# Moving the sigmoid-weighted gates of a conformer/attention block from the convolution stage into the attention stage, on one NeuronCore

## The chip, the core and the metric

The kernel runs on one core of a Trainium2 chip. A core has a matmul engine (TensorE, "PE" in the profile; "PEld" is its loading of stationary operands), a vector engine (VectorE, "DVE"), an activation engine (ScalarE, "ACT"), GpSimd ("POOL") and a sync engine (SyncE, "SP"), which here only issues DMAs. Each engine runs its own list of instructions in order and waits on semaphores for the others. The metric is the device time of the one core in microseconds. Three runs of the kernel before the change took 1415.45, 1418.73 and 1419.97 us; the median is 1418.73.

## The reference

One layer, in fp32, on 1024 latent tokens and 256 context tokens of width 1024. Weights are split per branch from one input projection:

```python
h = rms_norm(x, g_pre) * (1.0 + sc) + sh               # adaLN modulation
ua, gate_a, q, k, v, gate_b, gm = split_proj(h @ w_in)
o = latent_attention(rope(rms_norm(q)), k_all, v_all)  # 16 heads, 4 kv heads, 1280 keys
y_attn = (o * silu(gate_b)) @ w_attn_out
a, g = split(ua)
y = depthwise_conv31(a * sigmoid(g)) + conv_b
y = silu(layer_norm(y, ln_g, ln_b)) * silu(gate_a)
y_conv = y @ w_conv_out
ga, gb = split(gm)
out = (sigmoid(ga) * y_conv + sigmoid(gb) * y_attn) @ w_out
x_new = x + gt * rms_norm(out, g_post)
```

## The kernel before

**Products.** fp32 products are made of three reduced-precision ones: an operand is split into a high part (ScalarE casts it, `whi`) and a low part (source minus high part, `wlo`, by VectorE or GpSimd), and `mm3` adds high*high, low*high and high*low in PSUM. Everything is held with channels on the 128 partitions and 512 tokens (half of the sequence) in the free dimension.

**Jobs and units.** The large input projection is a list of *jobs*. A job is 128 output channels; it has two halves of 512 tokens; a half is eight *units*, and a unit is one `mm3`, three matmuls of 128x512 (`proj`). So a job has 16 units. A half accumulates in one of two PSUM buffers (`ppj` in the rows) and is taken out by an *evacuation* after its eighth unit; the half after the next one can't start before that. There are four kinds of evacuation:

- convolution gate (`gate` in `conv_jobs`): ScalarE takes the tanh (`ts<-ppj`);
- convolution value (`value`): VectorE multiplies (`y<-ts,ppj`), and the 31 taps of the depthwise convolution of those channels are put in a list, `taps`;
- silu (`silu_job`, for `gate_a` into the DRAM tile `gaD` and for `gate_b` into `gbD`): ScalarE takes the tanh, then VectorE does (tanh + 1) * value from PSUM (`ts<-ts,ppj`), then SyncE stores;
- tanh (`tanh_job`, for the merge gates `gm`, into `tgaD` and `tgbD`): ScalarE takes the tanh, then SyncE stores. VectorE has no part in it.

`stream` runs the jobs one after the other and prefetches the weights of one job: two DMAs of 256 KB (`wraw`, two buffers), two casts, two low parts on the engine in `wl[0]` (`wparts`, lines 142 to 160). `filler(n)` runs n units, `pump(n)` issues n taps, and `work(n)` does n units with taps at a fixed rate.

**Stages.** In order: modulation and the first jobs (to about 80 us); the context's keys and values; the weights of the first attention group (`group_w(0)`, line 587: four pairs of DMAs, a cast `wgh` and a low part `wgl` for each); 16 steps of queries, keys and values (four groups `g`, four quarters `q`), each with 20 units of the projection between its parts; then the rest of the units up to number 464, while the taps run out; then the PSUM is dealt out anew (`pump(len(taps))`, `unshare(2)`, `share({"o": 1})`, `share({"s": 5})`, lines 1441 to 1444): the two banks in which VectorE gathers the convolution (`pconv`) become part of the five buffers `ps` of the scores; then the maxima of the first window, and the attention proper: 16 windows of 20 steps, each with two score matmuls, an exponential on ScalarE, sums on GpSimd and VectorE, maxima of the next window on VectorE, and one unit of projection. The normalisation of the convolution's output and its gate (`ln_var`, `z_prep`) run beside the attention and read `gaD`; `gate_load` reads `gbD` for each pair of heads. After the attention comes the output: two levels of block products by a scheme with seven products for eight, and the last norm.

**What sets the order.** From the start up to the end of the 16 steps the four engines keep the order of the program text (`held = True`); after that (line 1429 on) a scheduler orders the instructions of each engine by priority, and what stands under `urgent()` comes early. SyncE's DMAs are ordered by the scheduler throughout.

**Order of the jobs.** 45 jobs are made in `early` (line 1316 on): 14 for the convolution with ten others dealt in between them, and the rest after them. The 15 silu jobs come first among the others, and the 16 tanh jobs after them; the first 29 jobs are units 0 to 464, so all silu jobs are through before the PSUM is dealt out anew, and all tanh jobs come after it, mostly in the attention.

Of the kernel before, what the change touches and what calls it, by code (L numbers as in the profile page):

```python
# [22 lines left out]
KD = 8  # L23
# [11 lines left out]
def block_kernel(ctx: ExitStack, tc: tile.TileContext, x, cx, cc, wmod, bmodT, bmodg, vecs, gpost,  # L35
# [18 lines left out]
    PE, V, S, G = (Ordered(e) for e in (nc.tensor, nc.vector, nc.scalar, nc.gpsimd))  # L54
# [7 lines left out]
    def nm(s):  # L62
        cnt[0] += 1
        return f"{s}_{cnt[0]}"

    def tl(tag, shape, bufs, dtype=F32, pool="sb"):
        return pools[pool].tile(list(shape), dtype, tag=tag, bufs=bufs, name=nm(tag))

    def opened(name, side="left"):
        p = tc.tile_pool(name=nm(name), bufs=1, side=side, reuse_waits="tile")  # L70
        pools[name] = p.__enter__()
        return p
# [35 lines left out]
    def split(hi, lo, src, he=None, le=None):  # L108
        if he is V or he is G:
            he.tensor_copy(hi, src)  # L110
        else:
            S.copy(hi, src)
        return (le or V).tensor_tensor(out=lo, in0=src, in1=f32(hi), op=ALU.subtract)
# [28 lines left out]
    wl = [G]  # L142
# [17 lines left out]
    def proj(w, rhs, hf, evac, tag="pj"):  # L160

        his, los = w
        p = pt(tag)
        for k in range(KD):
            mm3(p[:], his[k // 4][:, k % 4, :], los[k // 4][:, k % 4, :], rhs[k][0][hf][:], rhs[k][1][hf][:],
                k == 0, k == KD - 1)
            if k == KD - 1:
                with urgent():
                    evac(p, slice(hf * 512, hf * 512 + 512))
            yield  # L170
# [287 lines left out]
    def rope_tables():  # L458
        tcos, tsin = tl("blk", (P, NT, 32), 4, pool="A"), tl("blk", (P, NT, 32), 4, pool="A")
        SP.dma_start(out=tcos[:], in_=rcos)  # L460
        SP.dma_start(out=tsin[:], in_=rsin)
        gq = tl("blk", (P, NT, 32), 4, pool="A")[:, 0:4, :].rearrange("p (i a) b -> p i (a b)", i=2)
        SP.dma_start(out=gq[:, 0, :], in_=qg.partition_broadcast(P))
        SP.dma_start(out=gq[:, 1, :], in_=kg.partition_broadcast(P))
        yield 6
        for i in range(2):
            CC = tl("rope", (P, NT, HD), 4, pool="A")
            SS = tl("rope", (P, NT, HD), 4, pool="A")
            for hh in range(2):
                a, b = hh * 32, (1 - hh) * 32  # L470
                V.tensor_tensor(out=CC[:, :, a:a + 32], in0=tcos[:, :, 0:32],
                                in1=gq[:, i, a:a + 32].unsqueeze(1).to_broadcast([P, NT, 32]), op=ALU.mult)
                V.scalar_tensor_tensor(out=SS[:, :, a:a + 32], in0=tsin[:, :, 0:32], scalar=(1.0 if hh else -1.0),
                                       in1=gq[:, i, b:b + 32].unsqueeze(1).to_broadcast([P, NT, 32]),
                                       op0=ALU.mult, op1=ALU.mult)
                yield 2
            rope.append((CC, SS))
# [7 lines left out]
    gaD = [dram.tile([P, T], F32, name=nm("gaD")) for _ in range(KD)]  # L485
    tgaD = [dram.tile([P, T], F32, name=nm("tgaD")) for _ in range(KD)]
    tgbD = [dram.tile([P, T], F32, name=nm("tgbD")) for _ in range(KD)]
    ogD = [dram.tile([P, T], F32, name=nm("ogD")) for _ in range(KD)]
    gbD = [dram.tile([P, T], F32, name=nm("gbD")) for _ in range(KD)]
# [97 lines left out]
    def group_w(g):  # L587
        gw[g] = [], []
        raws = []

        def load(k):
            raws.append(tl("wgr", (P, 2, 384), 4, pool="wg"))
            SP.dma_start(out=raws[-1][:, :, 0:128], in_=wkv[:, k:k + 2, g * 128:(g + 1) * 128])
            SP.dma_start(out=raws[-1][:, :, 128:384], in_=wq[g, :, k:k + 2, :])
        for k in range(0, KD, 2):
            load(k)
        yield 6 if g else 10
        for k in range(0, KD, 2):
            hi, lo = tl("wgh", (P, 2, 384), 4, F32R, "wg"), tl("wgl", (P, 2, 384), 4, F32R, "wg")
            split(hi[:], lo[:], raws[k // 2][:], le=G if g else V)  # L600
            for i in range(2):
                gw[g][0].append(hi[:, i, :])
                gw[g][1].append(lo[:, i, :])
            yield 2 if g else 4
# [244 lines left out]
    def tanh_job(src, dst):  # L849
        def ev(p, tok):  # L850
            t = tl("ts", (P, 512), 4)
            S.activation(t[:], p[:], AF.Tanh, scale=0.5)
            SP.dma_start(out=dst[:, tok], in_=t[:])
        return src, lambda w, hf: proj(w, hT, hf, ev)

    def silu_out(p, dst):
        t = tl("ts", (P, 512), 4)
        S.activation(t[:], p[:], AF.Tanh, scale=0.5)
        V.scalar_tensor_tensor(out=t[:], in0=t[:], scalar=1.0, in1=p[:], op0=ALU.add, op1=ALU.mult)
        SP.dma_start(out=dst, in_=t[:])  # L860

    def silu_job(src, dst):
        return src, lambda w, hf: proj(w, hT, hf, lambda p, tok: silu_out(p, dst[:, tok]))
# [279 lines left out]
    def conv_out_job(j):  # L1143
        def ev(p, tok):
            t = tl("ts", (P, 512), 4)
            SP.dma_start(out=t[:], in_=tgaD[j][:, tok])
            V.scalar_tensor_tensor(out=t[:], in0=t[:], scalar=1.0, in1=p[:], op0=ALU.add, op1=ALU.mult)
            SP.dma_start(out=mcD[j][:, tok], in_=t[:])
        return wco[j], lambda w, hf: proj(w, zt, hf, ev)
# [163 lines left out]
                fin(*{2: (0, 1), 3: (1, 5), 4: (2, 7)}[n])  # L1313


    gate_jobs = [silu_job(wch[16 + j], gaD[j]) for j in range(1, KD)]
    gate_jobs += [silu_job(wch[24 + j], gbD[j]) for j in range(KD)]
    tanh_jobs = [tanh_job(wch[32 + j], tgaD[j]) for j in range(KD)]
    tanh_jobs += [tanh_job(wch[40 + j], tgbD[j]) for j in range(KD)]
    early = gate_jobs[0:1]  # L1320
    for j in range(1, KD):
        early += conv_jobs(j)
        for _ in range(2 - j % 2):
            early.append(gate_jobs[len(early) - 2 * j])
    early += gate_jobs[len(early) - 2 * (KD - 1):] + tanh_jobs
    zjobs = [conv_out_job(j) for j in range(KD)]
    NF = 16 * len(early)
    nj = len(early)
# [13 lines left out]
    def filler(n):  # L1342
        done[0] += n
        return run(fill, n)
# [3 lines left out]
    def work(n):  # L1348

        for _ in range(n):  # L1350
            filler(1)
            owed[0] = min(owed[0] + RATE, 3.0)
            while owed[0] >= 1:
                pump(1)
                owed[0] -= 1
# [18 lines left out]
    closed(stp)  # L1374
    app = opened("A")
    wgp = opened("wg")
    bg = rope_tables()
    next(bg)
    ones_rows()
    for d in group_w(0):  # L1380
        work(d)
    prev = None
    per = (NF - done[0] - NB - 72) // 16
# [2 lines left out]
    for g in range(NG):  # L1386
        for q in range(4):
# [14 lines left out]
            for i in range(per):  # L1402
# [13 lines left out]
                if i == due:  # L1416
                    d = next(bg, None)
# [11 lines left out]
    closed(app)  # L1429
    for e in (V, S, G):  # L1430
        e.held = False
    wl[0] = V
    bpp = opened("B")
    load_group(0)
    for w in range(2):
# [20 lines left out]
    score(0, 0)  # L1456
    score(0, 1)

    late = {}

    def later(step, gen):
# [15 lines left out]
    for i in range(2 * NS):  # L1477
# [24 lines left out]
        for g in late.pop(i, []):  # L1502
            with tc.issue_after(crit[0].ins), urgent():
                d = next(g, None)
# [113 lines left out]
```

## Time and profile before

| | us |
|---|---|
| median of three runs | 1418.73 (1415.45 to 1419.97) |
| the profiled execution | 1418.84 |
| its span, first to last instruction | 1417.0 |
| what lies around the span | 1.84 |
| TensorE busy | 1353.8 (96% of the span) |
| VectorE busy | 1028.2 (73%) |
| ScalarE busy | 565.1 (40%) |
| GpSimd busy | 699.7 (49%) |
| mean granted TensorE clock | 0.987 of full speed |

A busy share of 96% says that TensorE is the bound on average. The places where it is not are read from three views: the waits of TensorE in a stretch of the span (who it waited for, the sum, how often, the longest), the table by stretches of time with the granted clock beside the busy time, and the instructions in order of time, in which a bracket at the end of a row gives the idle time before it and the instruction that ended it. A granted clock of 0.50 means that the engine ran at 1.2 GHz instead of 2.4.

### The profile page before, as it was taken

To read this page: it belongs to the slowest core of one execution; us is meant where nothing else is said; L and a number is where in the kernel's file an instruction comes from. 1 tells how busy PE (TensorE), PEld (TensorE's weight loads), DVE (VectorE), ACT (ScalarE), POOL (GpSimd) and SP (SyncE) were. 2 spreads that over 40 slices of the span, in tenths; PEclk is the share of its full clock that TensorE was granted. 3 is DMA by queue.
4 is the path that set the end of the run, shared out by engine and by line. 5 is a ranking of instruction groups with operands and counts; after the bars stand their busy time and mean duration, and the time that the engine had idled before them with its cause. 6 is when DMAs were issued, how large, how long until landed. Compare 5 with 4: busy or idle time off the path is not lost.

```text
span 1417.0 us, 19558 instructions
## 1 busy us (share of the span) xinstructions
PE 1353.8 (96%) x6520; PEld 1003.5 (71%) x6520; DVE 1028.2 (73%) x1523; ACT 565.1 (40%) x1397; POOL 699.7 (49%) x567
## 2 busy tenths in 40 slices
PE   5999899999999999799999999999999999999996
PEld 3767789897888887566656666666665655788774
DVE  4486888898988898856764666667576675449977
ACT  5541344334343432144444444444454434222233
POOL 2121247566656550046665565556546666362623
PEclk9999999999999999999999999999999999999998
DMA  9733435444444447514544444543355658699754
GB/s 340 253 112 89 138 108 164 164 141 148 138 145 147 145 140 204 157 51 134 187 154 129 128 149 147 155 146 127 112 190 161 223 186 267 215 315 343 250 188 153
DMA packets 153332, 242.45 MB, mean 171 GB/s; under 512 B 19936, under 2 KB 72716, under 8 KB 153232
## 3 DMA queue, kind: packets, MB, share of 16 engines
q1 hardware_dynamic: 139792, 218.07, 46.9%
q10 hardware_dynamic: 13440, 23.14, 5.6%
q8 instruction: 51, 0.84, 0.2%
q14 instruction: 49, 0.40, 0.1%
HBM read 161.50 MB, written 79.52 MB: 170 GB/s over the span
## 4 chain that ended last, share of the span: by engine, by line
PE 60%; DVE 13%; issue 5%; DMA 4%; POOL 4%; ACT 3%; ACTq 1%; SPq 0%; POOLq 0%; DVEq 0%
PE ppj L50 27%; PE ps L50 16%; PE po L50 15%; DVE pconv L50 5%; PE pm L50 2%; DVE qkt L50 2%; DVE t L50 1%; DVE qk L50 1%; ACT pe L50 1%; DMA wraw<-in_wch 1%; POOL wlo L50 1%; DVE r1st L50 1%; POOL y L50 1%; DVE mx L50 1%; ACT qk L50 1%
## 5 line engine op out<-in xcount | busy, mean ns | idle before, releaser
L50 PE MATMUL ppj<-t,whi 128*128 128x512 f32 x1728 | 619.6, 403 | 14.9 <-DVE ts L50 11.3
L50 PEld LDWEIGHTS ppj<-t,whi 128*128 128x128 f32 x1728 | 328.4, 190 | 120.3 <-issue 34.0
L50 PE MATMUL ppj<-t,wlo 128*128 128x512 f32 x864 | 341.7, 395 | 0.0
L50 DVE TENSOR_REDUCE mx<-ps 128x1 f32<-128x512 f32 (+1 forms) x320 | 199.7, 681 | 119.2 <-PE ps L50 118.9
L50 ACT ACTIVATE pe<-ps 128x512 f32<-128x512 f32 x320 | 188.1, 597 | 204.5 <-PE ps L50 194.2
L50 PE MATMUL ps<-r,kk 128*128 128x512 f32 (+1 forms) x640 | 202.7, 398 | 1.5 <-DMA r<-mr 1.5
L50 POOL TENSOR_TENSOR psum<-psum,pe 128x512 f32<-128x512 f32 x128 | 175.4, 1387 | 41.3 <-ACT pe L50 36.6
L50 PEld LDWEIGHTS ppj<-t,wlo 128*128 128x128 f32 x864 | 164.9, 191 | 29.7 <-issue 0.2
L50 DVE SCALAR_TENSOR_TENSOR pconv<-y,cw,pconv 128x507 f32<-128x507 f32 (+5 forms) x224 | 167.9, 749 | 15.5 <-ACT pconv L50 9.6
L50 PE MATMUL po<-pe,vt 128*64 128x512 f32 x640 | 144.4, 597 | 0.0
L50 PEld LDWEIGHTS ps<-r,kk 128*128 128x128 f32 (+1 forms) x640 | 120.9, 189 | 31.1 <-issue 1.7
L50 POOL TENSOR_TENSOR psum<-psum,part 128x512 f32<-128x512 f32 x64 | 89.8, 1405 | 97.9 <-DVE part L50 97.9
L50 PE MATMUL po<-wgh,t 128*128 128x384 f32 x512 | 132.0, 339 | 0.0
L50 POOL TENSOR_TENSOR wlo<-wraw,whi 128x512 fp32r<-128x512 f32 x59 | 79.0, 1345 | 98.3 <-ACT whi L50 79.6
L50 PEld LDWEIGHTS po<-pe,vt 128*64 128x64 f32 x640 | 43.1, 136 | 81.2 <-issue 78.9
L50 PEld LDWEIGHTS po<-wgh,t 128*128 128x128 f32 x512 | 93.1, 188 | 1.7 <-ACT qk L50 0.4
L50 DVE SCALAR_TENSOR_TENSOR pconv<-y,cs,pconv 128x505 f32<-128x505 f32 (+7 forms) x120 | 90.0, 750 | 3.3
L50 DVE TENSOR_TENSOR wlo<-wraw,whi 128x512 fp32r<-128x512 f32 x53 | 50.8, 959 | 51.9 <-ACT whi L50 51.9
L50 POOL TENSOR_TENSOR psum<-pe,pe 128x512 f32<-128x512 f32 x32 | 42.3, 1342 | 89.5 <-ACT pe L50 89.5
L50 PE MATMUL po<-wgl,t 128*128 128x384 f32 x256 | 86.3, 337 | 0.0
L50 ACT CAST whi<-wraw 128x512 fp32r<-128x512 f32 x112 | 68.7, 632 | 32.6 <-PE ppj L50 17.3
L50 PE MATMUL ps<-kk,rq 64*128 64x512 f32 (+1 forms) x384 | 67.0, 406 | 13.4 <-issue 7.4
(221 smaller groups left out, 1830.9 us busy)
## 6 DMA issues: line engine op xcount, KB each, us to landing
wraw<-in_wch SPq DMA_DIRECT2D x96, 256.0 KB
opD<-opw SPq DMA_DIRECT2D x56, 256.0 KB
wm<-in_wmod SPq DMA_DIRECT2D x24, 512.0 KB
W<-opD SPq DMA_DIRECT2D x48, 256.0 KB
r1D<-r1st SPq DMA_DIRECT2D x32, 256.0 KB
y<-accD SPq DMA_DIRECT2D x16, 512.0 KB
r<-r1D ACTq DMA_DIRECT2D x32, 256.0 KB
opD<-acc SPq DMA_DIRECT2D x13, 512.0 KB
```

Of the source, the lines that this page charges most:

```text
L50: i = f(*a, **k)
```

## The change

Three edits. First, the order of the jobs: besides the convolution's jobs now stand two silu jobs (`gate_b`, 0 and 1) and then the 16 tanh jobs; the other 13 silu jobs come at the end of the list, in an order that mixes `gate_a` and `gate_b`. The number of jobs, 45, is as before. Second, the eight DMAs of `group_w(0)` are issued before those of the rotary tables and the rows of ones, and 16 units instead of 10 lie between them and the first split of these weights. Third, `wl[0] = V` moves from the end of the 16 steps to the first scores, so that the low parts of the projection's weights between these two places are made on GpSimd.

```diff
-        yield 6 if g else 10
+        yield 6 if g else 16
...
-    gate_jobs = [silu_job(wch[16 + j], gaD[j]) for j in range(1, KD)]
-    gate_jobs += [silu_job(wch[24 + j], gbD[j]) for j in range(KD)]
-    tanh_jobs = [tanh_job(wch[32 + j], tgaD[j]) for j in range(KD)]
-    tanh_jobs += [tanh_job(wch[40 + j], tgbD[j]) for j in range(KD)]
-    early = gate_jobs[0:1]
+    ga_job = lambda j: silu_job(wch[16 + j], gaD[j])
+    gb_job = lambda j: silu_job(wch[24 + j], gbD[j])
+    side = [gb_job(0), gb_job(1)] + [tanh_job(wch[32 + j], tgaD[j]) for j in range(KD)]
+    side += [tanh_job(wch[40 + j], tgbD[j]) for j in range(KD)]
+    early = side[0:1]
     for j in range(1, KD):
         early += conv_jobs(j)
         for _ in range(2 - j % 2):
-            early.append(gate_jobs[len(early) - 2 * j])
-    early += gate_jobs[len(early) - 2 * (KD - 1):] + tanh_jobs
+            early.append(side[len(early) - 2 * j])
+    early += side[len(early) - 2 * (KD - 1):]
+    early += [ga_job(1), gb_job(2), ga_job(2), ga_job(3), gb_job(3), ga_job(4), ga_job(5), gb_job(4), ga_job(6), ga_job(7),
+              gb_job(5), gb_job(6), gb_job(7)]
...
+    first_w = group_w(0)
+    d = next(first_w)
     bg = rope_tables()
     next(bg)
     ones_rows()
-    for d in group_w(0):
+    work(d)
+    for d in first_w:
         work(d)
...
         e.held = False
-    wl[0] = V
     bpp = opened("B")
...
     score(0, 1)
 
+    wl[0] = V
     late = {}
```

Where this moves instructions, the lists of three engines show it. On ScalarE, at the weights of the first group: `ts` is the tanh of a silu job's half, `wgh` a cast of the group's weights, which waits for their DMA, `whi` a cast of the projection's weights. Before:

```order
L50 ACTIVATE ts_1436<-ppj_1353 128x512
L50 CAST wgh_1455<-wgr_1395 128x768
L50 ACTIVATE ts_1473<-ppj_1440 128x512
L50 CAST wgh_1477<-wgr_1398 128x768
L50 CAST whi_1502<-wraw_1481 128x512
L50 CAST wgh_1506<-wgr_1401 128x768
```

and now:

```order
L50 ACTIVATE ts_1436<-ppj_1353 128x512
L50 ACTIVATE ts_1469<-ppj_1440 128x512
L50 CAST wgh_1487<-wgr_1384 128x768
L50 CAST whi_1498<-wraw_1473 128x512
L50 CAST wgh_1511<-wgr_1387 128x768
L50 CAST whi_1518<-wraw_1475 128x512
```

The tanh of the silu job's second half has moved ahead of the first cast of the group's weights.

On VectorE, near the end of the last taps (`pconv`), shortly before the first maxima: `ts` is the product of a silu job, `wlo` a low part of weights. Before:

```order
L50 SCALAR_TENSOR_TENSOR pconv_5526<-y_1049_5019,cs,pconv_5526 128x508
L50 SCALAR_TENSOR_TENSOR ts_5904<-ts_5904,ppj_5866 128x512
L50 SCALAR_TENSOR_TENSOR pconv_5526<-y_1049_5019,cs,pconv_5526 128x509
L50 SCALAR_TENSOR_TENSOR pconv_5526<-y_1049_5019,cs,pconv_5526 128x510
L50 TENSOR_TENSOR wlo_5967<-wraw_5949,whi_5966 128x512
L50 SCALAR_TENSOR_TENSOR pconv_5526<-y_1049_5019,cs,pconv_5526 128x511 x2
L50 SCALAR_TENSOR_TENSOR pconv_5526<-y_1049_5019,cs,pconv_5526 128x510
L50 SCALAR_TENSOR_TENSOR ts_5937<-ts_5937,ppj_5909 128x512
L50 TENSOR_TENSOR wlo_5993<-wraw_5951,whi_5992 128x512
```

and now:

```order
L50 SCALAR_TENSOR_TENSOR pconv_5512<-y_1048_4996,cs,pconv_5512 128x508
L50 SCALAR_TENSOR_TENSOR pconv_5512<-y_1048_4996,cs,pconv_5512 128x509
L50 SCALAR_TENSOR_TENSOR pconv_5512<-y_1048_4996,cs,pconv_5512 128x510
L50 SCALAR_TENSOR_TENSOR pconv_5512<-y_1048_4996,cs,pconv_5512 128x511 x2
L50 SCALAR_TENSOR_TENSOR pconv_5512<-y_1048_4996,cs,pconv_5512 128x510
```

The taps now follow one another with nothing between them. From the last low parts `r1st` of the queries to the end of the taps VectorE had 49 instructions and now has 34.

On VectorE again, in the attention, around step 50: `mx` is a maximum over scores in PSUM, `O` the product with a gate, `y` the centring of the convolution's output, `rc` a reciprocal, `part` a sum of two exponentials. Before:

```order
L50 TENSOR_TENSOR O_7254<-gate_7005,po_7039 128x512
L50 TENSOR_REDUCE mx_7113<-ps_7282 128x2
L50 TENSOR_REDUCE mx_7113<-ps_7283 128x2
L50 TENSOR_REDUCE mx_7113<-ps_7288 128x1
L50 TENSOR_REDUCE mx_7113<-ps_7289 128x1
L50 TENSOR_TENSOR y_1536_7167<-y_1536_7167,acc_6341 128x512
L50 RECIPROCAL rc_7308<-dc_7258 128x8
L50 TENSOR_TENSOR y_1536_7167<-y_1536_7167,acc_6341 128x512
```

and now:

```order
L50 TENSOR_TENSOR O_7232<-gate_6982,po_7016 128x512
L50 TENSOR_REDUCE mx_7090<-ps_7260 128x2
L50 TENSOR_REDUCE mx_7090<-ps_7261 128x2
L50 TENSOR_REDUCE mx_7090<-ps_7266 128x1
L50 TENSOR_REDUCE mx_7090<-ps_7267 128x1
L50 TENSOR_TENSOR y_1536_7145<-y_1536_7145,acc_6315 128x512
L50 SCALAR_TENSOR_TENSOR ts_7278<-ts_7278,ppj_7133 128x512
L50 TENSOR_TENSOR y_1536_7145<-y_1536_7145,acc_6315 128x512
L50 RECIPROCAL rc_7287<-dc_7236 128x8
```

A product of a silu job now stands between the attention's instructions; there are 26 such places, between the first window and the twelfth.

## Rows read from the trace of the kernel before

**Rows 1.** The page, first part: busy time, share of the span, instructions.
```profile
PE 1353.8 (96%) x6520; PEld 1003.5 (71%) x6520; DVE 1028.2 (73%) x1523; ACT 565.1 (40%) x1397; POOL 699.7 (49%) x567
```
**Rows 2.** Waits of PE, 0 to 150: sum in us, times, longest.
```profile
PE ppj L50 <- DVE ts L50: 6.9, 2, 5.2
```
**Rows 3.** Waits of PE, 150 to 525.
```profile
PE pm L50 <- DVE qk L50: 2.3, 1, 2.3
```
**Rows 4.** Waits of PE, 525 to 620.
```profile
PE ps L50 <- issue: 7.4, 1, 7.4
PE ppj L50 <- DVE ts L50: 3.7, 1, 3.7
```
**Rows 5.** Waits of PE, 620 to 1060.
```profile
PE ps L50 <- ACT pe L50: 2.4, 3, 1.5
```
**Rows 6.** In order of time, DVE, then PE, 579 to 586.
```profile
579.20 4.67 DVE L50 SCALAR_TENSOR_TENSOR pconv<-y,cs,pconv 128x509 f32<-128x509 f32 x6
583.90 0.75 DVE L50 SCALAR_TENSOR_TENSOR acc<-y,cs,pconv 128x512 f32<-128x512 f32 x1
...
584.75 1.19 PE L50 MATMUL ps<-kk,rq 64*128 64x512 f32 x3 [7.40 <-issue]
```
**Rows 7.** Stretches: length, busy PE, PEld, DVE, ACT, POOL (instructions), clock, DMA share, GB/s.
```profile
145.90:151.30 5.40, 5.38 (x13) 4.24 (x14) 3.76 (x5) 1.54 (x3) 1.56 (x3) 0.50 0.73 208
346.50:349.70 3.20, 3.20 (x11) 2.78 (x12) 3.06 (x5) 0.94 (x2) 2.64 (x5) 0.51 0.53 194
533.20:537.40 4.20, 4.20 (x15) 3.38 (x16) 4.02 (x6) 0.95 (x2) 0.00 (x0) 0.59 0.17 62
584.70:588.70 4.00, 3.95 (x10) 2.77 (x11) 2.43 (x4) 0.00 (x0) 2.36 (x1) 0.52 0.65 164
711.40:718.40 7.00, 7.00 (x16) 5.21 (x17) 5.69 (x7) 3.27 (x6) 4.38 (x5) 0.51 0.42 163
536.00:577.00 41.00, 40.89 (x179) 33.37 (x177) 34.38 (x52) 9.56 (x19) 1.29 (x1) 0.98 0.83 227
640.00:1010.00 370.00, 367.50 (x1777) 230.83 (x1777) 242.85 (x347) 169.35 (x286) 221.42 (x152) 0.99 0.47 145
```
**Rows 8.** In order of time, 134 to 146: start, length, engine, instruction.
```profile
134.38 0.38 SPq L460 DMA_DIRECT2D blk<-in_rcos  x1
...
136.70 0.44 SPq L593 DMA_DIRECT2D wgr<-in_wkv  x1
...
142.00 0.83 ACT L50 CAST wgh<-wgr 128x768 fp32r<-128x768 f32 x1 [9.59 <-issue]
142.74 0.59 ACT L50 ACTIVATE ts<-ppj 128x512 f32<-128x512 f32 x1
...
145.18 0.68 DVE L50 SCALAR_TENSOR_TENSOR ts<-ts,ppj 128x512 f32<-128x512 f32 x1
```
**Rows 9.** In order of time, DVE before PE's wait at 344.
```profile
336.74 0.69 DVE L50 SCALAR_TENSOR_TENSOR ts<-ts,ppj 128x512 f32<-128x512 f32 x1 [3.09 <-ACT ts L50]
```
**Rows 10.** Groups of DVE, 530 to 585: busy us, mean ns, idle before.
```profile
L50 DVE SCALAR_TENSOR_TENSOR ts<-ts,ppj 128x512 f32<-128x512 f32 x9 | 6.1, 682 | 0.4 <-ACT ts L50 0.3
L50 DVE TENSOR_TENSOR wlo<-wraw,whi 128x512 fp32r<-128x512 f32 x8 | 5.5, 688 | 5.3 <-ACT whi L50 5.3
```
**Rows 11.** In order of time, ACT, 574 to 578.
```profile
574.50 0.62 ACT L50 CAST whi<-wraw 128x512 fp32r<-128x512 f32 x1 [5.09 <-DMA wraw<-in_wch]
```
**Rows 12.** The page, costliest groups: low parts on GpSimd.
```profile
L50 POOL TENSOR_TENSOR wlo<-wraw,whi 128x512 fp32r<-128x512 f32 x59 | 79.0, 1345 | 98.3 <-ACT whi L50 79.6 <-DMA x<-in_wkv 17.7 <-issue 1.1
```
**Rows 13.** In order of time, DVE beside a busy GpSimd, then an idle one.
```profile
343.42 1.65 DVE L50 TENSOR_TENSOR qk<-qk,rope 128x512 f32<-128x512 f32 x1
...
346.26 5.47 DVE L50 SCALAR_TENSOR_TENSOR pconv<-y,cw,pconv 128x508 f32<-128x508 f32 x7
...
530.31 0.69 DVE L50 TENSOR_TENSOR qk<-qk,rope 128x512 f32<-128x512 f32 x1
```
**Rows 14.** Groups of DVE, 640 to 1010.
```profile
L50 DVE TENSOR_TENSOR wlo<-wraw,whi 128x512 fp32r<-128x512 f32 x24 | 26.5, 1106 | 30.5 <-ACT whi L50 30.5
```

## The prediction

> **What bounds the kernel now.** First the page: TensorE is busy for 96% of the span [rows 1], so only places where it waits or runs slowly can give time back, and work on other engines counts where it causes such a place. Then the waits of TensorE by stretch. Up to 150 us it waits 6.9 us for `ts` of VectorE, once 5.2 us [rows 2]; in the 16 steps once 2.3 us for the rotary part `qk` [rows 3]; after them 3.7 us for `ts` and 7.4 us for something that the profile doesn't name [rows 4]; in 440 us of attention only 2.4 us in three waits [rows 5]. The unnamed one is told by the order of time: TensorE starts again at 584.75, and VectorE ended the convolution's last instruction at 583.90 + 0.75 = 584.65 [rows 6]. That instruction empties the PSUM banks which the new `ps` buffers take over, so the wait is VectorE's, behind with its taps. Last the granted clock: behind each long wait TensorE runs for some microseconds at about half speed, 0.50 to 0.59, that is mostly at 1.2 GHz [rows 7]. A wait costs itself and that. One matmul of the projection at full clock takes 40.89 / 179 = 0.228 us [rows 7], a unit of three 0.685.
>
> So before the attention VectorE in its fixed order is what TensorE waits for, and in the attention TensorE is the bound.
>
> **The change part by part.** The sum is made against the profiled execution, 1418.84 us, 0.1 from the median.
>
> *A, the first group's weights.* On ScalarE the cast `wgh` waits for its DMA until 142.00, the tanh of the silu job stands behind it (142.74), and VectorE's product comes at 145.18 [rows 8]. TensorE needs that PSUM buffer and waits 5.2 us until 145.9, then runs 5.4 us at 0.50 [rows 2, 7]: 5.2 + 2.7 = 7.9. With 16 units ahead of the split the tanh of that half stands before the casts and waits for nothing new. Next late would be the half after the following one: its buffer is freed by a tanh behind two of the casts. The DMAs now go out where the tables' did, at 134.38 instead of 136.70 [rows 8], so the first cast is at about 142.0 - 2.3 = 139.7 and the second a microsecond or two later, while TensorE, which came to its wait at 145.9 - 5.2 = 140.7, is busy with the half between until 140.7 + 8 x 0.685 = 146.2. The eight DMAs pass only the tables and ones, which nobody needs for several steps. I take the whole 7.9; the other 1.7 of the 6.9 lies earlier and stays. Bounds: 4 (a shorter wait at the group's first product) to 7.9 + 1.7 = 9.6.
>
> *B, the 16 steps.* Nine silu jobs in them lose their VectorE product. At the one named wait, 2.3 us and 3.2 us at 0.51 (1.6), together 3.9 [rows 3, 7], VectorE had stood idle 3.09 us ahead of a silu product until ScalarE had the tanh, and the rotary part came after it [rows 9]. That product goes. Between nothing and 3.9 I take 3, since ScalarE's own lateness can still hold the rotary part.
>
> *C, the wait of 3.7 us.* A product `ts` stood behind rotary part and taps; the half that is there now needs ScalarE alone. With 4.2 us at 0.59 (1.7) [rows 4, 7] that is 5.4. Bounds 2 (another instruction in order is late) and 5.4; I take 5.4, as ScalarE is idle for most of that stretch (9.56 us busy of 41 [rows 7]).
>
> *D, the PSUM's new deal.* 7.4 us and 4.0 us at 0.52 (1.9) make 9.3 [rows 4, 7]. From 530 on VectorE loses its 8 remaining products of 0.682 (5.5 us; the ninth lies ahead of the wait of C) and 8 low parts (5.5), for whose cast it also stood idle 5.3: 16.3 in all [rows 10]. TensorE comes sooner, as six units were done before the 16 steps: 18 x 0.228 = 4.1. So the taps end 16.3 - 7.4 - 4.1 = 4.8 us before they are needed, and the wait is gone. Late next are the weights: the job behind the deal had its cast at 574.50 after 5.09 us of waiting for its DMA [rows 11]. With the cast (0.62) and a low part at GpSimd's 1.345 [rows 12] they are there at 576.5, and TensorE, which was at the deal at 584.7 - 7.4 = 577.3, now comes at 573.2: 3.3 us too early if the DMA is no sooner. It should be sooner by up to the products and low parts that stood ahead of the queries' last low parts (two of each, 2.7 us), since the queries' stores and loads, the DMAs in front of it, start with these. I take 1.3 us of wait and D = 8.0. Bounds: 9.3 - 3.3 - 1.6 (half clock as at B) = 4.4, and 9.3; nothing if VectorE's taps became slower.
>
> That last bound hangs on GpSimd beside VectorE. A two-input VectorE instruction on SBUF, the rotary product, took 1.65 us beside a busy GpSimd and 0.69 without; the taps, with one input in PSUM, took 5.47 / 7 = 0.78 beside it and 4.67 / 6 = 0.78 without [rows 6, 13]. The Trainium skill, "SBUF — State Buffer", section "Who interferes with whom", says that an instruction of VectorE with two SBUF inputs contends with a GpSimd instruction that reads SBUF, and one with a single SBUF input doesn't; the rows agree on both. By that rule the low parts on GpSimd could hold up the rotary part of the last quarter, and the sum would lose another 3.9, a wait like that of B: 1401. Since VectorE is ahead of its taps by then, I leave it 0.06 of the forecast's chance below.
>
> *E, the attention.* 26 products of 0.682 come in, 17.7 us of VectorE, between 640 and about 1010, where VectorE is busy 242.85 of 370 us (66%; it becomes 70%) and TensorE 367.50 [rows 7]. Behind a product in VectorE's list stand maxima and partial sums; they free the `ps` buffers for the next scores and feed GpSimd. One wait there was seen with its full price: 1.5 us for an exponential [rows 5] and then 7.0 us at 0.51 (3.4): 4.9 [rows 7]. Bounds: -4.9 (that wait goes too) to +17.7 (every product on TensorE's path). I take +3, over half of one more such wait: the nearest row is that of the 24 low parts of 1.106 us which stand in the same list now [rows 14]: 26.5 us, and TensorE hardly waits. What must not be late is met: the last `gate_a` job ends about four steps (some 7 us) before it is read, `gate_b` 8 steps or more.
>
> Sum: 7.9 + 3 + 5.4 + 8.0 - 3 = 21.3; 1418.84 - 21.3 = 1397.5. I say 1397.
>
> **The rivals.**
> 1. *A DMA takes VectorE's place at the deal.* For it: DMA is busy 0.83 of 536 to 577 [rows 7], and a cast waited 5.09 us for it. Against: its start moves up too. D falls to nothing: 1405.5. Chance 0.14.
> 2. *The attention pays.* Three more waits of 4.9 instead of 3 us: 1397.5 - 3 + 14.7 = 1409. For it: the one wait there already falls where VectorE carries `y`, `part` and `wlo` at once; against: 2.4 us in 440 [rows 5]. 0.10.
> 3. *Slower.* The same place carried further: a product in VectorE's list delays a maximum, the five `ps` buffers run out, and TensorE drops to half clock. Each time is 4.9; from 21.3 + 3 = 24.3, five times of 26, the gain is gone, and with seven the time is 1397.5 - 3 + 34.3 = 1429. 0.05.
> 4. *The silu products aren't why VectorE is late in the steps and after.* Then taps and rotary part keep the waits, and only A and half of C come: 1418.84 - 7.9 - 2.7 = 1408. Against: two of the named waits are for these products [rows 2, 4]. 0.05.
> 5. *All of it.* B and D whole, and the attention's wait gone: 1397.5 - 0.9 - 1.3 - 7.9 = 1387. 0.06.
>
> **How the numbers follow.** The forecast has 0.60, with 1390 to 1404 as its own range. A measurement of this kernel can tell about 0.3%, 4.3 us, from no change. The range of 1386 to 1411 takes in rivals 1, 2, 4 and 5 and leaves out the slow one and the tails of the others, together about 0.15. Faster by more than 0.3% (below 1414.5): the forecast, 1 and 5 whole, and most of 2 and 4, 0.89. Within 0.3%: 0.06. Slower: 0.05.
>
> **What would show it.** Right: no wait of TensorE over 1 us between 138 and 152, and clock 1.00 there; none for `ts` near 515; at the new deal VectorE's last `acc` ends before TensorE's first maxima, and no half clock behind it; in the attention 26 `ts` products of 0.68 and under 8 us of waits. A wrong step would be named by the waits of TensorE: `wlo` or `wraw` at the deal for rival 1, `mx`, `pe` or `part` in the attention with clocks near 0.5 for 2 and 3, `qk` in the steps for 4. The forecast is wrong if the span up to the first scores is not shorter by 15 us, or the attention is longer by over 10.

## The result, and the profile after

The changed kernel took 1404.3 us in the median of four runs (1400.34 to 1406.56); the kernel before, run beside it, 1419.35 us (1415.45 to 1422.44, four runs). The ratio is 0.9882, with a 95% interval from 0.9851 to 0.9913: by that ratio 16.7 us less (12.3 to 21.2), by the medians 15, where 21.3 had been forecast.

The profiled execution took 1406.56 us, with a span of 1404.8. The page, first part, answers to [rows 1]: VectorE lost 6 us, GpSimd gained 13, and TensorE has the same work. (L50 in the rows below is one helper line of the kernel, through which all instructions pass; the tile names tell them apart.)

```profile
PE 1353.0 (96%) x6520; PEld 1003.3 (71%) x6520; DVE 1022.3 (73%) x1513; ACT 564.3 (40%) x1397; POOL 712.5 (51%) x577
```

One correction comes first. Up to about 135 us both programs are the same, and still this execution was later there. The table by stretches (columns as in [rows 7]) shows most of the reason: first the changed kernel's stretch 20 to 40, then the same of the kernel before.

```profile
20.00:40.00 20.00, 16.50 (x98) 9.32 (x102) 9.60 (x19) 10.81 (x19) 4.58 (x5) 0.83 0.84 290
```
```profile
20.00:40.00 20.00, 16.72 (x119) 10.58 (x120) 10.46 (x20) 12.55 (x22) 5.50 (x6) 1.00 0.92 319
```

TensorE ran partly at 1.2 GHz there, in this execution and not in the other: 0.17 of 20 us are 3.4 us, and from 40 to 135 the mean clock was 0.98 against 1.00, another 1.9. Below, every profile is shifted so that TensorE's first resumption after a wait for `ts` falls on 135.00, where the kernel before has it. For the changed kernel it stands at 140.28, a shift of 5.28 us. Shifted so, the changed kernel gains 12.2 + 5.28 = 17.5 us of span.

The waits of TensorE in the changed kernel, for the stretches 0 to 150, 150 to 525, 525 to 620 and 620 to 1060, answer to [rows 2 to 5] (sum in us, times, longest):

```profile
PE ppj L50 <- DVE ts L50: 1.6, 1, 1.6
...
PE ppj L50 <- POOL wlo L50: 0.7, 2, 0.4
...
PE ps L50 <- DVE acc L50: 7.4, 1, 7.4
PE ppj L50 <- ACT ts L50: 0.4, 1, 0.4
...
PE ps L50 <- ACT pe L50: 2.4, 3, 1.5
```

The waits of 5.2, 2.3 and 3.7 us are gone. The one of 7.4 us at the PSUM's new deal stands there as large as before, now with a name: VectorE's `acc`, the end of the convolution. The stretches of the changed kernel that answer to [rows 7]: first the one around the first group's weights, then the 16 steps and the place of the 3.7 us, both now at full clock; the third lies behind the wait that stayed, the last is the attention:

```profile
140.00:150.00 10.00, 9.72 (x43) 8.02 (x44) 8.04 (x12) 4.56 (x8) 3.39 (x3) 1.00 0.94 303
152.00:530.00 378.00, 377.27 (x1883) 334.96 (x1882) 333.34 (x506) 153.72 (x664) 225.66 (x228) 1.00 0.45 145
...
571.10:575.20 4.10, 4.09 (x10) 2.86 (x11) 2.44 (x4) 0.00 (x0) 2.36 (x1) 0.50 0.75 170
640.00:1010.00 370.00, 367.61 (x1768) 232.66 (x1768) 255.35 (x368) 169.61 (x289) 220.54 (x152) 1.00 0.47 143
```

Now the place that did not follow the forecast, in order of time, VectorE and then TensorE (start, length, instruction, idle time before it):

```profile
556.80 0.75 DVE L50 SCALAR_TENSOR_TENSOR acc<-pconv,vec,y 128x511 f32<-128x511 f32 x1 [10.59 <-ACT y L50]
...
558.50 11.77 DVE L50 SCALAR_TENSOR_TENSOR pconv<-y,cs,pconv 128x505 f32<-128x505 f32 x15
570.31 0.75 DVE L50 SCALAR_TENSOR_TENSOR acc<-y,cs,pconv 128x512 f32<-128x512 f32 x1
...
571.11 1.22 PE L50 MATMUL ps<-kk,rq 64*128 64x512 f32 x3 [7.41 <-DVE acc L50]
```

VectorE did lose the products and low parts: its 15 taps run on end to end. But before them it stands idle for 10.59 us, until ScalarE has written `y`. ScalarE over that time (ACTq are the DMAs that it issues; a group's length includes the gaps in it):

```profile
539.09 5.44 ACTq L50 DMA_DIRECT2D r<-r1D  x4
...
545.07 0.60 ACT L50 ACTIVATE ts<-ppj 128x512 f32<-128x512 f32 x1 [5.82 <-DMA r<-r1D]
545.54 0.45 ACTq L50 DMA_DIRECT2D rq<-r1D  x1
550.04 0.45 ACTq L50 DMA_DIRECT2D r<-r1D  x1
550.59 0.62 ACT L50 CAST whi<-wraw 128x512 fp32r<-128x512 f32 x1 [4.92 <-DMA r<-r1D]
550.62 3.49 ACTq L50 DMA_DIRECT2D r<-r1D  x3
554.16 0.60 ACT L50 ACTIVATE ts<-ppj 128x512 f32<-128x512 f32 x1 [2.95 <-DMA vt<-vD]
556.09 0.62 ACT L50 CAST whi<-wraw 128x512 fp32r<-128x512 f32 x1 [1.33 <-DMA wraw<-in_wch]
556.14 0.33 ACTq L50 DMA_DIRECT2D gate<-gbD  x1
556.61 0.15 ACT L50 COPY y<-pconv 128x1 f32<-128x1 f32 x1
```

What VectorE waits for is the last of these rows: one column, 0.15 us, the end of `odd_end` (line 809). ScalarE is hardly busy; its list is held by DMAs that it issues, the rows `rq`, `r1` and `r2` of the first two windows, and for the last 1.33 us by a cast that waits for its weights. One issue lasts 0.33 to 0.55 us, but the next often comes microseconds later (545.54, then 550.04). In the program's list (number, instruction, the counters that it waits for) each of these twelve issues waits for counters of earlier DMAs, and the copy stands behind all of them:

```
513 L50 DMA r_1155_5654<-r1D_641 64x512 [waits DMAHW4_49]
514 L50 DMA r_1154_5653<-r1D_641 128x512 [waits DMAHW7_49,DMAHW6_49,Activation_49]
515 L50 DMA r_1157_5658<-r1D_642 64x512 [waits DMAHW5_49,DMAHW7_49,DMAHW3_49,DVE_49]
516 L50 DMA r_1156_5657<-r1D_642 128x512 [waits DMAHW1_49]
...
527 L50 COPY y_1048_4996<-pconv_5512 128x1 [waits DVE_49]
```

The list also tells which DMAs these are. The DMAs of SyncE and ScalarE raise eight counters in turn, and each of the twelve row loads waits until the eighth DMA before it has landed: for eight of them that is one of SyncE's (weights, keys, values, stores), for four an earlier row load.

The theory for the runs below: at the new deal neither VectorE's work nor the weights are late, but this copy, because it shares an in-order list with DMA issues that wait. The rivals: VectorE's own load; the DMA itself, which is busy all the time there and would be the next to be late; and that the copy had cost as much in the kernel before.

### The profile page after: what moved, and what is told of

It is laid out like the page before. It is cut to its first block, busy times and chain, and to the rows that moved or that the text cites. A ratio compares the mean times of both kernels' runs of the same rounds, so it can differ in the third digit from the quotient of the medians.

```text
span 1404.8 us, 19526 instructions
## 1 busy us (share of the span) xinstructions
PE 1353.0 (96%) x6520; PEld 1003.3 (71%) x6520; DVE 1022.3 (73%) x1513; ACT 564.3 (40%) x1397; POOL 712.5 (51%) x577
## 4 chain that ended last, share of the span: by engine, by line
PE 76%; DVE 9%; DMA 4%; ACT 3%; POOL 3%; issue 3%; ACTq 0%; SPq 0%; POOLq 0%; DVEq 0%
PE ppj L50 34%; PE po L50 21%; PE ps L50 17%; PE pm L50 4%; DVE pconv L50 3%; DVE t L50 2%; DMA wm<-in_wmod 1%; DVE mx L50 1%; DMA y<-in_wout 1%; ACT pe L50 1%; POOL y L50 1%; POOL wgl L50 1%; DMA r<-r1D 1%; ACTq L50 0%; DVE acc L50 0%
## 5 line engine op out<-in xcount | busy, mean ns | idle before, releaser
L50 PE MATMUL ppj<-t,whi 128*128 128x512 f32 x1728 | 617.7, 402 | 4.6 <-DVE t L50 2.6
L50 PEld LDWEIGHTS ppj<-t,whi 128*128 128x128 f32 x1728 | 328.1, 190 | 107.7 <-issue 33.7
L50 PE MATMUL ppj<-t,wlo 128*128 128x512 f32 x864 | 341.8, 396 | 0.7 <-POOL wlo L50 0.7
L50 DVE TENSOR_REDUCE mx<-ps 128x1 f32<-128x512 f32 (+1 forms) x320 | 199.5, 681 | 105.3 <-PE ps L50 104.8
L50 ACT ACTIVATE pe<-ps 128x512 f32<-128x512 f32 x320 | 187.9, 597 | 205.1 <-PE ps L50 188.0
L50 PE MATMUL ps<-r,kk 128*128 128x512 f32 (+1 forms) x640 | 202.8, 398 | 0.4 <-DMA r<-mr 0.3
L50 POOL TENSOR_TENSOR psum<-psum,pe 128x512 f32<-128x512 f32 x128 | 173.9, 1375 | 41.9 <-ACT pe L50 38.1
L50 PEld LDWEIGHTS ppj<-t,wlo 128*128 128x128 f32 x864 | 164.8, 191 | 31.5 <-POOL wlo L50 1.8
L50 DVE SCALAR_TENSOR_TENSOR pconv<-y,cw,pconv 128x507 f32<-128x507 f32 (+5 forms) x224 | 168.0, 750 | 19.6 <-ACT pconv L50 13.4
L50 POOL TENSOR_TENSOR wlo<-wraw,whi 128x512 fp32r<-128x512 f32 x69 | 91.3, 1331 | 138.2 <-ACT whi L50 90.3
L50 PE MATMUL po<-pe,vt 128*64 128x512 f32 x640 | 144.4, 597 | 0.0
L50 PEld LDWEIGHTS ps<-r,kk 128*128 128x128 f32 (+1 forms) x640 | 121.3, 190 | 30.1 <-DMA r<-mr 0.7
L50 POOL TENSOR_TENSOR psum<-psum,part 128x512 f32<-128x512 f32 x64 | 89.1, 1394 | 105.1 <-DVE part L50 105.1
L50 PE MATMUL po<-wgh,t 128*128 128x384 f32 x512 | 131.7, 338 | 0.0
L50 PEld LDWEIGHTS po<-pe,vt 128*64 128x64 f32 x640 | 43.1, 136 | 81.2 <-issue 79.2
L50 PEld LDWEIGHTS po<-wgh,t 128*128 128x128 f32 x512 | 92.9, 188 | 1.3
L50 DVE SCALAR_TENSOR_TENSOR pconv<-y,cs,pconv 128x505 f32<-128x505 f32 (+7 forms) x120 | 90.0, 750 | 3.6
L50 PE MATMUL po<-wgl,t 128*128 128x384 f32 x256 | 86.3, 337 | 0.0
L50 ACT CAST whi<-wraw 128x512 fp32r<-128x512 f32 x112 | 69.1, 630 | 37.4 <-DMA wraw<-in_wch 17.7
L50 POOL TENSOR_TENSOR psum<-pe,pe 128x512 f32<-128x512 f32 x32 | 42.4, 1344 | 75.0 <-ACT pe L50 75.0
L50 PE MATMUL ps<-kk,rq 64*128 64x512 f32 (+1 forms) x384 | 66.5, 406 | 13.8 <-DVE acc L50 7.4
L50 DVE TENSOR_TENSOR part<-pe,pe 128x512 f32<-128x512 f32 x64 | 68.2, 1068 | 13.6 <-ACT pe L50 13.5
```

Source lines behind the costliest of these rows:

```text
L50: i = f(*a, **k)
```

## The experiments

Two sets of four kernels were run, each set on one chip beside the kernel before, which took 1424.13 us there in the first set and 1424.77 in the second (medians). Their ratios are to that; the changed kernel's is from its own measurement, beside 1419.35. The table has the shifted times of all profiles: of TensorE's first score, against that of the kernel before, and from there to the last product of the attention.

| kernel | ratio, 95% interval | shift | first score | against before | attention |
|---|---|---|---|---|---|
| before | | 0 | 607.0 | | 611.2 |
| changed | 0.9882 [0.9851, 0.9913] | -5.28 | 588.5 | -18.5 | 611.9 |
| before, job order only | 0.9905 [0.9873, 0.9938] | -6.00 | 595.6 | -11.4 | 611.6 |
| before, first group's weights only | 0.9912 [0.9893, 0.9931] | -4.67 | 599.6 | -7.4 | 610.9 |
| before, low parts only | 0.9967 [0.9945, 0.9989] | -1.93 | 605.6 | -1.4 | 613.3 |
| before, copy on VectorE | 0.9969 [0.9946, 0.9992] | -0.31 | 606.5 | -0.5 | 608.1 |
| changed, copy on VectorE | 0.9797 [0.9768, 0.9826] | +0.74 | 578.5 | -28.5 | 611.3 |
| changed, rows on SyncE | 0.9781 [0.9746, 0.9816] | -0.43 | 578.9 | -28.1 | 612.1 |
| changed, both of these | 0.9782 [0.9756, 0.9809] | -2.92 | 578.8 | -28.2 | 609.9 |
| changed, more work in the silu products | 0.9924 [0.9902, 0.9947] | -4.80 | 588.7 | -18.3 | 622.1 |

A shifted time is that of one execution of each kernel, and the kernel before was profiled once, when it took 1418.84 us. By the ratios the edits to the kernel before gave more than by the shifted times: 12.5 us (9.8 to 15.2) for the first group's weights, where the first score came 7.4 sooner, 4.7 (1.6 to 7.8) for the low parts and 4.4 (1.1 to 7.7) for the copy. So the table says where the time went, and differences of up to some 5 us between kernels stay open in it.

**The copy on VectorE.**

```diff
-            S.copy(O[:, 511:512], acc[:, 1, 511:512])
+            V.tensor_copy(O[:, 511:512], acc[:, 1, 511:512])
```

> The changed kernel, with the copy of the last column in odd_end (128x1) on VectorE instead of ScalarE. Theory (the wait of 7.4 us at the PSUM's new deal stayed because VectorE stood idle 10.6 us for that copy, which stood in ScalarE's list behind casts and DMA issues that waited for DMA): VectorE goes on with its taps at once, the taps end some 10 us sooner, TensorE's wait of 7.4 us and the half clock behind it (about 2 us) go, less up to 1 us of wait for weights: about 8 us less than the changed kernel, 1396 us. Rival (the stretch is bound by DMA: without VectorE's wait the weights or the loads of queries and keys hold TensorE as long): within 2 us of the changed kernel, 1404, and the wait at the deal is then for wlo, wraw or r.

Measured: 1393.57 us in the median (1390.64 to 1397.64, six runs). ScalarE is held as before; VectorE no longer waits for it. Waits of TensorE from 525 to 620, then ScalarE, VectorE and TensorE in order of time, in this kernel:

```profile
PE ppj L50 <- ACT ts L50: 0.5, 1, 0.5
PE ps L50 <- DMA r<-mr: 0.3, 1, 0.3
```
```profile
532.88 5.80 ACTq L50 DMA_DIRECT2D r<-r1D  x4
...
540.20 0.16 DVE L50 COPY y<-pconv 128x1 f32<-128x1 f32 x1
540.28 0.74 DVE L50 SCALAR_TENSOR_TENSOR acc<-pconv,vec,y 128x511 f32<-128x511 f32 x1
...
553.77 0.75 DVE L50 SCALAR_TENSOR_TENSOR acc<-y,cs,pconv 128x512 f32<-128x512 f32 x1
...
557.28 0.73 PE L50 MATMUL ps<-kk,rq 64*128 64x512 f32 x4
```

The wait at the deal is gone, and `acc` ends 2.8 us before TensorE's first maxima (557.28 - 554.52). The first score is 10.0 us earlier than in the changed kernel. The rival, that the DMA would be the next to be late, falls: the DMA share was 1.05 in 540 to 560 here and 1.02 in the changed kernel, that is busy throughout, and TensorE waited for no weights.

**The rows on SyncE.** Who issues the twelve DMAs; the copy stays on ScalarE.

```diff
-        max_load(w)
-        row_load(w)
+        max_load(w, SP)
+        row_load(w, SP)
```

> The changed kernel, with the query loads of the first two windows (rq, r1, r2) issued on SyncE instead of ScalarE. Theory (ScalarE's list is held by its DMA issues, 5.4 and 3.5 us, and the copy stands behind them): ScalarE reaches the copy sooner, VectorE's idle time of 10.6 us falls below 5, and the wait at the deal falls from 7.4 us to between 0 and 3: 1396 to 1401 us. Rival (ScalarE is held by the cast that waits for its weights, not by the issues): the idle time stays near 10 us, the wait near 7, 1404 us, or more where SyncE's weight loads now stand behind the query loads.

Measured: 1391.32 us (1388.34 to 1394.56, four runs). ScalarE's copy and VectorE's instruction behind it, and the first two of the issues, now on SyncE:

```profile
541.34 0.16 ACT L50 COPY y<-pconv 128x1 f32<-128x1 f32 x1 [2.01 <-DVE y L50]
...
541.53 0.75 DVE L50 SCALAR_TENSOR_TENSOR acc<-pconv,vec,y 128x511 f32<-128x511 f32 x1 [0.23 <-ACT y L50]
...
540.21 1.10 SPq L893 DMA_DIRECT2D rq<-r1D  x2
```

The order is turned round: ScalarE now waits 2.01 us for VectorE, and the copy comes at once. The row loads go out no sooner in total: the first at 540.21, the last at 551.11. What counts is whose list they stand in, since SyncE computes nothing. The time is below the forecast 1396 to 1401, as the whole wait went and not a part of it. With the experiment above this shows the cause from both ends: either the instruction that is waited for leaves the list, or what holds the list does.

**Both edits.** The diffs are those of the two above.

> The changed kernel with the one-column copy on VectorE and also with the loads of rows of the first two windows asked for by SyncE and not by ScalarE. Theory: either edit removes the same wait of 7.4 us, so that both give no more than 2 us beyond either alone, some 1390 to 1393 us and a ratio to the kernel before of 0.977 to 0.980; no wait of TensorE over 1.5 us between 525 and 620. Rival: the two add up, ScalarE's free time moves the casts and the tanh jobs too, and the time falls by another 5 us or more, to a ratio below 0.975.

Measured: 1393.17 us (1390.31 to 1398.74, four runs), the same ratio as either alone. They cure one wait, once; ScalarE's freed time shows no further gain. All three kernels are some 2% faster than the kernel before and 1% faster than the changed one (their intervals lie apart from its own, which was measured apart from them), and the one-line edit is enough.

**The copy on VectorE in the kernel before.** The same line as above.

> The kernel before with one edit: the copy of one column at the odd window's end (128x1) is done by VectorE and not by ScalarE. Theory: in the kernel before a low part stands in VectorE's list just ahead of the instruction that needs that column, and waits 3.06 us for a cast which is held on ScalarE by the same DMA issues; so the copy alone gives nothing there, within 2 us of the kernel before, and the wait of 7.4 us stays. Rival: the copy cost as much in the kernel before as in the changed one, and the time falls by 8 us.

Measured: 1419.12 us (1415.91 to 1426.99, nine runs), and a first score 0.5 us earlier. By the ratio it is 4.4 us less (1.1 to 7.7), more than the 2 us of the theory; the attention of the profiled execution was 3.1 us shorter, and the cause of that stays open. First the kernel before at this place, ScalarE and then VectorE:

```profile
558.57 5.46 ACTq L50 DMA_DIRECT2D r<-r1D  x4
565.10 0.62 ACT L50 CAST whi<-wraw 128x512 fp32r<-128x512 f32 x1 [6.57 <-DMA r<-r1D]
...
565.75 0.69 DVE L50 TENSOR_TENSOR wlo<-wraw,whi 128x512 fp32r<-128x512 f32 x1 [3.06 <-ACT whi L50]
```

Now this kernel's VectorE, and its wait of TensorE at the deal:

```profile
561.64 0.75 DVE L50 SCALAR_TENSOR_TENSOR y<-y,cw,pconv 128x511 f32<-128x511 f32 x1
565.86 0.69 DVE L50 TENSOR_TENSOR wlo<-wraw,whi 128x512 fp32r<-128x512 f32 x1 [3.47 <-ACT whi L50]
566.47 0.15 DVE L50 COPY y<-pconv 128x1 f32<-128x1 f32 x1
```
```profile
PE ps L50 <- DVE acc L50: 7.1, 1, 7.1
```

In the kernel before another instruction, a low part of VectorE, waits there for a cast on the same held list. Its 3.06 us are part of the 5.3 us of idle time in [rows 10], and here, without the copy, it waits 3.47. So ScalarE's hold was in the trace of before, under another name, and removing one of the two instructions that it held up gave 0.5 us at the first score, while the same edit is worth 10.0 us there once the other is gone.

**The low parts alone.**

```diff
-    wl[0] = V
     bpp = opened("B")
...
+    wl[0] = V
```

> The kernel before with one edit: the low part of the weight chunk that VectorE still formed before the attention goes to GpSimd (wl[0] = V left out at that place). Theory (VectorE is held by ScalarE, not by its own work): in the kernel before, VectorE ended the tap y at 562.69 and the 0.15 us copy that it needs next came from ScalarE only at 565.62, behind the issue of four DMAs; so of the 8 low parts (5.5 us) and their 5.3 us of waiting only what lies behind that copy comes back, about two low parts: the wait of 7.4 us before the first maxima falls to between 5 and 7, the waits of 5.2, 2.3 and 3.7 us stay, and the time is 0 to 4 us below the kernel before. Rival (VectorE's own load makes the deal late): the wait falls by 7.4, and the time by 8 us or more.

Measured: 1420.06 us (1412.08 to 1423.9, eight runs). Waits of TensorE from 525 to 620, then VectorE:

```profile
PE ppj L50 <- DVE ts L50: 4.5, 2, 3.7
PE ps L50 <- issue: 3.8, 1, 3.8
```
```profile
568.17 0.75 DVE L50 SCALAR_TENSOR_TENSOR acc<-pconv,vec,y 128x511 f32<-128x511 f32 x1 [4.58 <-ACT y L50]
```

The wait at the deal fell by 3.6 us, more than the theory had (0.4 to 2.4); shifted, the first score came only 1.4 us earlier, since the waits for `ts` grew by 0.8 there, and by 1.4 between 150 and 525 (2.2 in place of 0.8). The theory is right in kind: low parts and their waiting are gone, and 4.58 us of them come back as a wait for the copy.

**The first group's weights alone.**

```diff
-        yield 6 if g else 10
+        yield 6 if g else 16
...
+    first_w = group_w(0)
+    d = next(first_w)
```

> The kernel before with one edit: the first group's weights are asked for ahead of the tables, and 16 units of products stand before them in place of 10. Theory: the wait of 5.2 us near 141 and its half clock go (7.9 us), but TensorE comes sooner to the deal of the PSUM while VectorE doesn't, so that part of it (the 4.1 us of the six units that are done ahead) stands there as a longer wait: 7.4 becomes about 11, and the time is 4 us below the kernel before. Rival: all of the 7.9 us is kept, since VectorE too starts its convolution sooner, and the wait at the deal stays at 7 to 8 us.

Measured: 1412.93 us (1411.04 to 1416.01, four runs). Waits of TensorE in 0 to 150, 150 to 525 and 525 to 620:

```profile
PE ppj L50 <- DVE ts L50: 1.7, 1, 1.7
...
PE ppj L50 <- POOL wlo L50: 3.1, 2, 2.7
...
PE ps L50 <- issue: 9.0, 1, 9.0
```

My theory fell here, and the rival held in the time: 7.4 of the 7.9 us are kept at the first score. It did not hold in its wait, which was to stay at 7 to 8 us: the one at the deal grew by 1.6 us to 9.0. Between 150 and 525 the waits of the kernel before, 2.3 us for the rotary part [rows 3] and twice 0.8, are gone, and 3.1 us for low parts came in their place, one of them 2.7; the cause of these stays open.

**The job order alone.** The lists of the change, without its other two edits.

> The kernel before with the new order of the jobs alone (first group's weights and low parts as before). Theory (the silu products were why VectorE was late in the 16 steps and at the 3.7 us wait): both of these waits go with their half clock, 2.3 + 1.6 + 0.8 + 5.4, about 10 us less than before, 1409 us; the first group's 5.2 us wait stays, and the wait at the deal stays within 3 us of 7.4. Rival (these waits went by the early group weights, which shift all later work by six units): 1419 us with a wait for qk or ts left in the steps.

Measured: 1409.38 us (1408.21 to 1414.66, five runs). Waits in 150 to 525 (this execution meets the first group's wait after 150), then in 525 to 620:

```profile
PE ppj L50 <- DVE ts L50: 5.9, 1, 5.9
...
PE pm L50 <- DVE qk L50: 0.5, 1, 0.5
...
PE ps L50 <- DVE acc L50: 5.6, 1, 5.6
```
```profile
562.67 0.69 DVE L50 TENSOR_TENSOR wlo<-wraw,whi 128x512 fp32r<-128x512 f32 x1 [5.31 <-ACT whi L50]
```

The wait of 3.7 us goes by this edit alone, and that for the rotary part falls from 2.3 to 0.5 us. That 1409 was met is in part luck, as the kernel before took 1424 beside it: by the ratio the edit gave 13.5 us (8.8 to 18.1). The last row is VectorE's low part in front of the instruction that reads the copied column. It waited 3.06 us in the kernel before and waits 5.31 here; with the low parts alone gone the copy is waited for 4.58 us, and with all three edits 10.59. The more is taken from VectorE, the longer it waits for the same held list.

The three edits alone give 11.4 + 7.4 + 1.4 = 20.2 us at the first score, all together 18.5. By the ratios they give 13.5 + 12.5 + 4.7 = 30.7, against 16.7 for the change, which was measured apart from them; whether they add up is not shown.

**More work in the silu products of the attention.** Each of the 26 products after the first scores is followed by two multiplications by one on VectorE, 52 in all.

```diff
+        if twice[0]:
+            V.tensor_scalar_mul(t[:], t[:], 1.0)
+            V.tensor_scalar_mul(t[:], t[:], 1.0)
```

> The changed kernel, with two more VectorE instructions (a multiplication by 1 of 128x512 in SBUF, about 0.45 us each) behind each of the 26 silu products of the attention: 52 x 0.45 = 23 us more of VectorE there, against the 17.7 us that the products themselves cost. Theory (VectorE has room in the attention; the products cost TensorE about 1 us in all): at most 3 us more than the changed kernel, 1404 to 1407 us. Rival (VectorE's list is close to holding the scores back): waits of TensorE for pe or mx with half clock behind them, 5 us each, three or more: 1419 us or more.

Measured: 1413.51 us (1404.23 to 1416.45, ten runs). The profiled execution is the slowest of the ten, and its attention is 10.2 us longer than the changed kernel's; by the ratios the difference is some 6 us, with intervals that overlap. VectorE's added instructions in 640 to 1010, this kernel's waits of TensorE in 620 to 1060, and its stretch:

```profile
L50 DVE TENSOR_SCALAR ts<-ts 128x512 f32<-128x512 f32 x46 | 41.7, 906 | 0.6
```
```profile
PE ps L50 <- ACT pe L50: 3.9, 5, 1.5
PE ps L50 <- DVE mx L50: 2.3, 3, 1.0
```
```profile
640.00:1010.00 370.00, 364.82 (x1727) 228.31 (x1726) 289.97 (x407) 165.09 (x280) 219.64 (x149) 0.98 0.46 142
```

Each added instruction took 0.906 us in the mean (0.37 to 1.98) and not 0.45, so that far more than the products themselves came in: 41.7 us in these 370. The theory had at most 3 us and the rival 15 or more; the size lies between them. Late maxima appear as a wait that the changed kernel did not have, 2.3 us in three, and the clock falls from 1.00 to 0.98. So VectorE had idle time for the 16 us of products that the change moved in, and in this execution no longer for 42 more: at 290 of 370 us busy, some of its instructions are on TensorE's path.

## Why the prediction was right and wrong

The time, 1404.3, lies in the range, 7 us above the forecast, and that owes something to luck: the largest step, D, failed whole, 8.0 us, and B and E came out 2.6 and 2.3 us better than taken. Of the prediction's own signs two failed at the deal, where `acc` ended after TensorE had come and half the clock stood behind it. The third, a span to the first scores shorter by 15 us, fails as it stands (607.0 to 593.8, 13.2 us) and is met only with the shift (18.5). By its steps, in shifted times:

- **A, right.** Taken 7.9. In the kernel before, the products of the first group began at 151.21 with 76 units of projection done, in the changed one at 152.69 - 5.28 = 147.41 with 82. Six units at 0.685 are 4.1 us, so 151.21 + 4.1 - 147.41 = 7.9. The cast was forecast at about 139.7; it stands at 144.82 - 5.28 = 139.5. Alone the edit kept 7.4.
- **B, too small.** Taken 3 of 3.9. TensorE was at the deal at 571.11 - 7.41 - 5.28 = 558.4 instead of 577.3: 18.9 us sooner, of which 7.9 are A and 5.4 are C, so B is some 5.6. The wait for the rotary part went whole, 2.3 us and its half clock of 1.6, and with it two waits between 150 and 525 that the sum had not counted, 0.8 us each for `y` and `ts`; 0.7 us for low parts came in. That makes 4.8 of the 5.6. I had taken ScalarE's own lateness off the 3.9, and it did not show.
- **C, right.** Taken 5.4; the wait is gone. The 0.4 us that TensorE waits for a tanh stand later, at 554.80, for the tanh that ScalarE's held list brings at 554.16.
- **D, failed.** Taken 8.0 of 9.3; it gave nothing. The step that failed is "16.3 in all, so the taps end 4.8 us before they are needed". It counted VectorE's instructions and the waits of its low parts, and took it that VectorE, without them, would run through. It did not ask for what else of ScalarE VectorE waits in that stretch. The low part's idle time in [rows 10] was read as a property of the low parts; it was ScalarE's list, held by DMA issues, and it passed to the next instruction that needed ScalarE, at 10.59 us instead of 3.06. With this wait removed, the taps end 2.8 us before they are needed, where 4.8 had been taken, the deal gave 10.0 us, a little over the 9.3 of the rows, and the 1.3 us that I had kept for late weights did not appear.
- **E, too dear.** Taken -3; the attention took 611.9 us against 611.2, and the four kernels with the job order of before differ by more than that (608.1 to 613.3). It cannot be told from nothing. The nearest row, that of the low parts in [rows 14], had said this, and the price of one more wait was put on top without a reason in the rows.

So 7.9 + 5.6 + 5.4 + 0 - 0.7 = 18.2 of the 21.3, against 17.5 us of span; the 5.6 of B is what A and C, taken whole, leave over. Rival 1, with D at nothing, had 1405.5 and so the right time for a wrong reason: TensorE waited for no weights. What it had right is that DMA set the pace, but by way of the issues on ScalarE, and only for what stands in ScalarE's list.

The rotary product of the last quarter did meet GpSimd's low parts, as the rule in "SBUF — State Buffer" of the Trainium skill, section "Who interferes with whom", has it: 1.66 us in the changed kernel beside them (the row below), 0.69 in [rows 13]. TensorE did not wait for it, so the sum lost nothing.

```profile
522.43 1.66 DVE L50 TENSOR_TENSOR qk<-qk,rope 128x512 f32<-128x512 f32 x1
```

Left open: whether another order of the DMAs, so that the eighth one before each row load lands sooner, would free the list; that was not tried.

## What to carry to other kernels

When an engine is relieved, ask for each instruction that it still has in that stretch what it waits for, down to the smallest, and what stands ahead of that on the other engine: idle time that the profile books on one instruction passes on to the next one that needs the same engine. DMAs issued from a computing engine stand in its in-order list with their waits; before a stretch where something of that engine is needed, issue them from SyncE, or do the small thing on the engine that needs it. And an edit that gives little alone (0.5 us at the first score for the copy) can be worth 10 us after another one, so it should be tried again there.

## What the runs showed of the hardware that was not expected

- Twelve row loads, each issued in 0.33 to 0.55 us, held ScalarE's computing for most of 539 to 556. The Trainium skill, "DMA: Bandwidth & Descriptors", section "Issuing engines are not separate DMA queues", says that DMAs of several engines share the same DMA engines, and that issuing from several saves only the sequencer's time to issue, usually small beside the DMA itself. Here it saved 9.6 us at the first score (588.5 to 578.9), because the issues' waits left ScalarE's list too.
- The first 135 us, with the same program, came out up to 6.7 us apart in the profiled executions (134.26 to 141.00), with clocks from 1.00 down to 0.83 in 20 to 40. Two profiles can't be compared by their spans without that shift.
- Half clock behind a wait lasts unequally long. Behind the wait of 1.5 us at 698 in the changed kernel the clock was at 0.50 for some 3 us and back at 1.00 from 702 on, as the two stretches below show; behind one like it in the kernel before it was 0.51 for 7.0 us [rows 7]. A price of 4.9 us for such a wait, as E and two rivals had it, is the dearer of the two.

```profile
700.00:702.00 2.00, 2.00 (x6) 1.60 (x5) 0.05 (x1) 0.60 (x1) 2.00 (x2) 0.50 0.20 75
702.00:705.00 3.00, 3.00 (x14) 2.41 (x13) 2.11 (x4) 2.19 (x4) 1.08 (x2) 1.00 0.31 89
```
